# The first MLP's second matrix: three quarters with stationary activations, a sum by tokens, and a turn back to features

## The chip, the core and the metric

The kernel runs on one core of one Trainium2 chip. The metric is the device time of one launch in microseconds (us), weights read from HBM included. The input is one sequence of 256 tokens with 2048 features, in float32.

## What is computed

A two-layer trunk. Each layer has a mixer and an MLP, both behind a modulated norm, and both added to the stream through a gate. The change touches the MLP of layer 0 alone:

```
h = rms_norm(x, norm_mlp_w) * (1 + sc2) + sh2        # 256 x 2048
a = relu(h @ w1) ** 2                                # w1: 2048 x 8192
x = x + g2 * (a @ w2)                                # w2: 8192 x 2048, one gate g2 per feature
```

The gate is a number for each output feature, the same for all tokens. So the gate may be put on the whole sum `a @ w2` or on each part of it.

## The kernel before

The stream `x` lies in SBUF by features: four tiles `x[0..3]` of 128 partitions x 4 x 256, a partition for a feature, the 256 tokens along the row. All weights come from HBM in loads of 1 MB (128 x 2048 float32), each the work of one *item*. To keep float32 precision at TensorE's faster format, each half of a load is split into a high part `wh` (ScalarE, a cast, L342) and a low part `wl` (VectorE, load minus high part, L346); activations are split likewise when they are made. An item multiplies high by high, high by low and low by high.

There are three kinds of item. `c_item` (L592) holds 128x128 of weights stationary and moves the activations: its `wh` products move high and low activations together (512 columns), its `wl` products the high ones alone (256 columns). The output has features on partitions, as `x` has. `a_item` (L554) holds 128x128 of activations stationary and moves 512 columns of weights; its output has tokens on partitions. `b_item` is not used in the MLP.

The MLP (`mlp`, L1516) has four passes `f` over 2048 of the 8192 hidden features. In each pass eight blocks of two `c_item`s make the hidden features (first matrix, evacuated by `relu2`), then eight blocks of two `c_item`s multiply them by the second matrix. After each such block `residual` (L951) adds the gated PSUM tile to `x` with four VectorE instructions (L958). One pass is thus 32 items, 16 of each matrix.

Beside this, the vectors of modulation (`sc`, `sh`, `g` of later norms) are made on VectorE: `mod_job` (L452) loads 1 MB into the same four `raw` buffers as the weights and multiplies and sums it with one instruction (L466). In layer 0's MLP 0.377 of such steps is put out per tick (L1561), four ticks to an item, which comes to about three of these loads to four of weights.

The order of the work is set as the program is written: `emit` (L252) loads item n+1 and then writes the products of item n; `tick` (L236) steps queued generators between pieces of an item, those in `self.fast` first, those in `self.bg` in turn. A scheduler then fixes one order for each engine and for SyncE's DMA queue, and each engine goes through its row strictly in that order: an instruction that waits holds all behind it. There are four `raw` buffers, four `wh` halves, five `wl` halves (two items' worth) and two large PSUM tiles.

Of the kernel before, what the change touches and what calls it, by code (L numbers as in the profile page):

```python
# [10 lines left out]
F32 = mybir.dt.float32  # L11
# [3 lines left out]
ALU = mybir.AluOpType  # L15
# [3 lines left out]
P = 128  # L19
D = 2048  # L20
SEQ = 256
# [91 lines left out]
class Trunk:  # L113
# [332 lines left out]
    def mod_start(self, layer):  # L446

        mix, mlp = ("mix", layer), ("mlp", layer)
        for v, key in enumerate((mix, mix, mix, mlp, mlp, mlp)):
            self.mod[v % 3, key] = self.const([P, 16], f"mod{layer}{v}")  # L450
# [497 lines left out]
        return get  # L948


    def residual(self, ps, cb, key, last, final=False, fs=(0, 1)):  # L951

        nc = self.nc
        self.need(2, key, 2 * cb + 2)
        g, x, b = self.mod[2, key], self.x[cb // 2], cb % 2
        for f in fs:
            for n in range(2):
                self.last = nc.vector.scalar_tensor_tensor(x[:, 2 * b + f], ps[:, f, n], g[:, 2 * cb + f : 2 * cb + f + 1], x[:, 2 * b + f], op0=ALU.mult, op1=ALU.add)  # L958
# [557 lines left out]
    def mlp(self, layer, acts, after=None):  # L1516

        nc = self.nc
        w1, w2 = self.i["w1"][layer], self.i["w2"][layer]
        NF = DFF // 2048  # L1520

        def relu2(ps, early):
            p = self.unit(F32R, [P, 2, 2, SEQ])
            lo = self.s2([P, 2, SEQ], tag="rs")
            nc.scalar.copy(lo, ps[:, :, 1])  # L1525
            nc.vector.tensor_tensor(lo, ps[:, :, 0], lo, op=ALU.add)  # L1526
            if early:
                self.early_add(lo)
            yield
            rl = self.s2([P, 2, SEQ], tag="rl")  # L1530
            nc.scalar.activation(rl, lo, AF.Relu)
            nc.scalar.activation(rl, rl, AF.Square)
            self.split(rl, p[:, :, 0], p[:, :, 1])
            return p

        half = lambda n: acts(n // 2)[0][n % 2]
        for f in range(NF):
            a = {}

            def sink(ps, cb, f=f, a=a):  # L1540
                a[cb % 8] = self.evac(relu2(ps, cb == 0), 1)
                if cb == 7:
                    self.mlp_rate(layer)

            if f == 0:
                self.first_blocks(w1, (0, 1, 2), half, sink)
            for cb in range(3 if f == 0 else 0, 8):
                self.c_blocks(w1, (f * 8 + cb,), half, sink)
            for cb in range(8):
                if f == NF - 1 and cb == 6:  # L1550
                    self.still = 4
                self.c_blocks(w2, (cb,), lambda n, a=a: a[n].finish(),
                              lambda ps, cb, fs=(0, 1), f=f: self.residual(ps, cb, ("mlp", layer), f == NF - 1, layer == 1 and f == NF - 1, fs), f * 2,
                              f == NF - 1 and cb == 7)
        if after is None:
            self.drain()
        else:
            self.early_item(after)

    def mlp_rate(self, layer):  # L1560
        self.rate = 0.377 if layer == 0 else 0.25  # L1561
# [226 lines left out]
def pack(inputs):  # L1788

    f = lambda n: np.asarray(inputs[n])  # L1790
    c = np.ascontiguousarray

    def chunks(w, width=512):
        k, n = w.shape
        nk = 2048 // width
        return c(w.reshape(k // (nk * P), nk, P, n // width, width).transpose(0, 3, 2, 1, 4)).reshape(k // (nk * P), n // width, P, 2048)
# [16 lines left out]
        "w1": np.stack([chunks(w, 256) for w in f("mlp_w1")]), "w2": np.stack([chunks(w, 256) for w in f("mlp_w2")]),  # L1813
    }


# [27 lines left out]
```

## Time and profile before

| | us |
|---|---|
| median of 3 runs | 2692.02 (2691.77 to 2692.03) |
| the profiled execution's own time | 2691.54 |
| its span, first to last instruction | 2689.8 |
| TensorE busy in the span | 2635.2 (98%) |
| VectorE busy | 2151.9 (80%) |
| ScalarE busy | 1348.2 (50%) |
| layer 0's MLP, second norm to end of the fourth pass | about 580 to 1290 of the span |

Times inside the span count from its first instruction. A row of the view by line names line, engine, operation, output<-inputs, count, busy time and the mean of one; `PEld` is the loading of a stationary operand, `SPq` the queue on which SyncE issues DMAs. In the timeline, neighbouring like instructions are drawn together: start, length of the stretch, what, xcount, and in brackets the idle time before and who ended it. The view by windows gives, for a stretch, the busy time of each engine, TensorE's granted clock (PEclk), the mean busy share of the 16 DMA engines and the rate.

### The profile page before, as it was taken

How to read it: one execution, taken by the hardware profiler on the slowest of the kernel's cores; microseconds unless marked ns; L12 is line 12 of the kernel's file. 1: busy time of each engine (PE TensorE's matmuls, PEld its weight loads, DVE VectorE, ACT ScalarE, POOL GpSimd, SP SyncE). 2: the span in 40 equal slices, each digit the busy share in tenths (PEclk: the TensorE clock that was granted, in tenths of full speed). 3: DMA queues.
4: the chain of work that ended last, by engine and by line, in shares of the span. 5: the costliest groups of instructions: out<-in, count | busy, mean ns of one | idle time of the engine just before them, and what ended most of it. 6: DMA issues, size and time to landing. Idle time of an engine off the chain costs nothing.

```text
span 2689.8 us, 40012 instructions
## 1 busy us (share of the span) xinstructions
PE 2635.2 (98%) x15834; PEld 2324.1 (86%) x15834; DVE 2151.9 (80%) x3106; ACT 1348.2 (50%) x1990; POOL 24.3 (1%) x98
## 2 busy tenths in 40 slices
PE   5999999999999999999999999999999999999999
PEld 4887989988888888888888888888888888888888
DVE  7998998997888888889889876888797855555554
ACT  3445455456345354454556544655455354453452
POOL 1000000000000000000000000000000000000000
PEclk9999999999999999999999999999999999999999
DMA  9986487868899898988566655655567855555553
GB/s 344 352 327 234 170 307 275 322 235 293 313 345 328 328 332 330 333 331 312 179 207 220 219 204 185 207 175 188 208 236 293 325 188 188 188 188 188 191 193 134
DMA packets 100459, 680.08 MB, mean 253 GB/s; under 512 B 11184, under 2 KB 14512, under 8 KB 19376
## 3 DMA queue, kind: packets, MB, share of 16 engines
q1 hardware_dynamic: 95376, 669.07, 68.6%
q10 hardware_dynamic: 4896, 8.46, 1.0%
q8 instruction: 124, 2.03, 0.3%
q14 instruction: 63, 0.52, 0.1%
HBM read 675.33 MB, written 2.16 MB: 252 GB/s over the span
## 4 chain that ended last, share of the span: by engine, by line
PE 90%; DVE 7%; ACT 2%; issue 1%; DMA 1%; DVEq 0%; SPq 0%; ACTq 0%
PE pw L332 71%; PE pg L332 12%; PE pm L335 3%; PE pm L332 2%; DVE wl L346 2%; DVE mraw L466 2%; PE pm L339 1%; DVE u L1619 0%; ACT wh L342 0%; DVE hf L893 0%; DVE u L1017 0%; DMA raw<-in_w_ab_dram 0%; ACT pm L1075 0%; DVE u L896 0%; ACT pm L1218 0%
## 5 line engine op out<-in xcount | busy, mean ns | idle before, releaser
L346 DVE TENSOR_TENSOR wl<-raw,wh 128x1024 fp32r<-128x1024 f32 x870 | 1053.8, 1223 | 433.4 <-ACT wh L342 430.9
L342 ACT CAST wh<-raw 128x1024 fp32r<-128x1024 f32 x870 | 905.0, 1050 | 980.8 <-PE pw L332 676.6
L332 PE MATMUL pw<-u,wh 128*128 128x512 f32 x5584 | 1318.8, 391 | 2.6 <-DVE u L896 1.3
L332 PEld LDWEIGHTS pw<-u,wh 128*128 128x128 f32 x5584 | 1032.5, 188 | 209.3 <-issue 1.9
L332 PEld LDWEIGHTS pw<-u,wl 128*128 128x128 f32 x5584 | 702.1, 191 | 21.0 <-DVE wl L346 1.1
L332 PE MATMUL pw<-u,wl 128*128 128x256 f32 x5584 | 711.0, 283 | 0.7 <-DVE wl L346 0.7
L466 DVE SCALAR_TENSOR_TENSOR mraw<-mraw,crow 128x2048 f32<-128x2048 f32 x192 | 438.8, 2287 | 8.6 <-DMA mraw<-in_mod_dram 8.4
L332 PE MATMUL pg<-wh,u 128*128 128x512 f32 x864 | 282.1, 398 | 0.0
L332 PEld LDWEIGHTS pg<-wh,u 128*128 128x128 f32 x864 | 162.0, 188 | 33.2 <-issue 1.0
L958 DVE SCALAR_TENSOR_TENSOR x<-pw,mod,x 128x256 f32<-128x256 f32 x352 | 161.9, 480 | 32.4 <-PE pw L332 30.0
L332 PE MATMUL pg<-wl,u 128*128 128x512 f32 x432 | 169.7, 393 | 0.4 <-DVE wl L346 0.2
L332 PE MATMUL pg<-u,wh 128*128 128x256 f32 x672 | 124.5, 286 | 0.0
L332 PEld LDWEIGHTS pg<-u,wh 128*128 128x128 f32 x672 | 105.5, 192 | 0.3
L332 PEld LDWEIGHTS pg<-wl,u 128*128 128x128 f32 x432 | 81.3, 188 | 18.2 <-DVE wl L346 1.9
L332 PE MATMUL pg<-u,wl 128*128 128x256 f32 x336 | 95.6, 284 | 0.1
L332 PE MATMUL pm<-u,wh 128*128 128x256 f32 (+1 forms) x340 | 64.1, 292 | 19.2 <-ACT wh L342 19.2
L332 PEld LDWEIGHTS pm<-u,wh 128*128 128x128 f32 x340 | 54.3, 199 | 20.3 <-ACT wh L342 20.0
L332 PEld LDWEIGHTS pg<-u,wl 128*128 128x128 f32 x336 | 64.4, 192 | 0.3 <-DVE wl L346 0.3
L1017 DVE SCALAR_TENSOR_TENSOR u<-pad,cst,u 128x256 f32<-128x256 f32 x144 | 61.6, 481 | 1.0 <-ACT u L1011 0.7
L1525 ACT COPY rs<-pw 128x512 f32<-128x512 f32 x64 | 36.8, 576 | 34.5 <-PE pw L332 34.5
L895 ACT ACTIVATE u<-hf,mod 128x256 fp32r<-128x256 f32 x64 | 29.3, 501 | 47.2 <-DVE hf L893 47.2
L1526 DVE TENSOR_TENSOR rs<-pw,rs 128x512 f32<-128x512 f32 x64 | 43.9, 686 | 9.9 <-ACT rs L1525 9.9
(298 smaller groups left out, 1520.5 us busy)
## 6 DMA issues: line engine op xcount, KB each, us to landing
raw<-in_w_dram SPq DMA_DIRECT2D x256, 1024.0 KB, 5.4
mraw<-in_mod_dram SPq DMA_DIRECT2D x192, 1024.0 KB, 6.3
raw<-in_w_ab_dram SPq DMA_DIRECT2D x56, 1024.0 KB, 6.3
raw<-in_w_ssd_dram SPq DMA_DIRECT2D x48, 1024.0 KB, 4.8
raw<-in_w_sz_dram SPq DMA_DIRECT2D x32, 1024.0 KB, 4.9
raw<-in_wo_ssd_dram SPq DMA_DIRECT2D x32, 1024.0 KB, 4.9
raw<-in_wo_ab_dram SPq DMA_DIRECT2D x16, 1024.0 KB, 6.0
sE<-sd_rowd ACTq DMA_DIRECT2D x32, 256.0 KB, 3.9
```

The costliest lines, as they stand in the source:

```text
L332: return self.nc.tensor.matmul(o, a, b, start=start, stop=stop, skip_group_check=True)
L335: self.nc.tensor.matmul(o, lhsT, rhs, start=True, stop=True, skip_group_check=True)
L339: return self.nc.tensor.transpose(o, a, self.anti if flip else self.ident[:k, :k])
L342: a = self.nc.scalar.copy(hi, src)
L346: b = self.nc.vector.tensor_tensor(lo, src, hi.bitcast(F32), op=ALU.subtract)
L466: x = nc.vector.scalar_tensor_tensor(raw, raw, 1.0, self.crow, op0=ALU.mult, op1=ALU.mult, accum_out=t[:, f : f + 1])
L895: nc.scalar.activation(hi, h[:, f], AF.Identity, bias=shift[:, col])
L958: self.last = nc.vector.scalar_tensor_tensor(x[:, 2 * b + f], ps[:, f, n], g[:, 2 * cb + f : 2 * cb + f + 1], x[:, 2 * b + f], op0=ALU.mul ...
L1017: nc.vector.scalar_tensor_tensor(h, pad[:, f, 1 + q : 257 + q], w[:, q, j : j + 1], h, op0=ALU.mult, op1=ALU.add)
L1525: nc.scalar.copy(lo, ps[:, :, 1])
L1526: nc.vector.tensor_tensor(lo, ps[:, :, 0], lo, op=ALU.add)
```

## The change

Of layer 0's second matrix, passes 0, 1 and 2 are done with `a_item`s (`w2_sums`): four groups `n` of 512 output features, each over four items and one PSUM tile. Pass 3 stays with `c_item`s and `residual`, and layer 1 stays as it was. The weights of passes 0 to 2 are packed 512 wide (`w2a`) and those of pass 3 256 wide (`w2b`).

The ungated sums of the three passes are kept by tokens, in the SBUF tiles of `x` itself (`tok` is another view of them). For this `x` is copied to HBM once, in pass 0 (`save_x`, four DMAs). Pass 0's sums are copied into the tiles by ScalarE, those of passes 1 and 2 added by VectorE (`add_sums`). Once group `n` of pass 2 is summed, `to_features(n)` runs as a background task: four VectorE transposes (32x32 squares inside 128x256), eight DMAs that put the squares into HBM in pieces of 128 bytes, one DMA that brings the saved `x[n]` back, eight DMAs that read the turned sums in pieces of 1 KB (`xz`), and four VectorE instructions that gate them and add them to `x[n]`. All DMAs go on SyncE's queue.

```diff
+    def save_x(self):
+        self.kept = [self.dram_p.tile([P, 4, SEQ], F32, tag=f"xk{n}", name=f"x_kept{n}") for n in range(4)]
+        for n in range(4):
+            self.nc.sync.dma_start(self.kept[n], self.x[n])
+            yield
...
+    def add_sums(self, ps, n, first):
+        for t in range(2):
+            if first:
+                self.nc.scalar.copy(self.tok(n)[:, t], ps[t])
+            else:
+                self.nc.vector.tensor_tensor(self.tok(n)[:, t], ps[t], self.tok(n)[:, t], op=ALU.add)
+
+    def to_features(self, n, key):
...
+        for t in range(2):
+            ys.append(self.s2([P, 512], tag="xy"))
+            for h in range(2):
+                c = slice(256 * h, 256 * h + 256)
+                nc.vector.transpose(ys[t][:, c], self.tok(n)[:, t, c])
+            yield
+        for t in range(2):
+            for q in range(4):
+                nc.sync.dma_start(scr[:, :, 4 * t + q], ys[t][32 * q : 32 * q + 32].rearrange("p (m i) -> p m i", i=32))
+        nc.sync.dma_start(self.x[n], self.kept[n])
+        for _ in range(5):
+            yield
+        cells = scr.rearrange("j (f a) b i -> j f a (b i)", a=4)
+        zs = [self.s2([P, 2, SEQ], tag="xz") for _ in range(2)]
+        for a in range(4):
+            for h in range(2):
+                nc.sync.dma_start(zs[h][32 * a : 32 * a + 32], cells[:, 2 * h : 2 * h + 2, a])
+        for _ in range(4):
+            yield
+        for f in range(4):
+            x = self.x[n][:, f]
+            nc.vector.scalar_tensor_tensor(x, zs[f // 2][:, f % 2], self.mod[2, key][:, 4 * n + f : 4 * n + f + 1], x, op0=ALU.mult, op1=ALU.add)
...
+            if layer == 0 and f < NF - 1:
+                self.w2_sums(self.i["w2a"], f, NF, lambda n, a=a: a[n].finish(), ("mlp", layer))
+                continue
...
+    def w2_sums(self, w, f, nf, act, key):
+        for n in range(4):
...
+            def after(n=n, ps=ps):
+                self.add_sums(ps, n, f == 0)
+                if f == nf - 2:
+                    self.turned.append(self.back(self.to_features(n, key)))
+            for k in range(4):
+                self.a_item(get, w[4 * f + k, n], lambda k=k: ([act(2 * k), act(2 * k + 1)], None), k == 0, k == 3, after if k == 3 else None)
```

The orders below are of pass 2 (the third), around its middle. Rows of the changed program carry its own line numbers (L968 is `add_sums`, L980 the transposes, L984, L985 and L992 the DMAs of `to_features`, L997 its gated add); the number behind a tile's name tells tiles of one name apart.

TensorE before, one block of the second matrix (two items): first the `wh` products (512 columns) and the `wl` products (256 columns) of one load, then those of the next, 64 matmuls in all.

```order
L332 MATMUL pw_9923<-u_8956,wh_9868 128x512 x4
L332 MATMUL pw_9923<-u_9055,wh_9868 128x512 x4
L332 MATMUL pw_9923<-u_9153,wh_9872 128x512 x4
L332 MATMUL pw_9923<-u_9252,wh_9872 128x512 x4
L332 MATMUL pw_9923<-u_8956,wl_9869 128x256 x4
L332 MATMUL pw_9923<-u_9055,wl_9869 128x256 x4
L332 MATMUL pw_9923<-u_9153,wl_9873 128x256 x4
L332 MATMUL pw_9923<-u_9252,wl_9873 128x256 x4
```

TensorE now, the first half of the first item of group 2 (two halves make an item of 24 matmuls, all with 512 columns).

```order
L332 MATMUL pg_9662<-wh_9614,u_8649 128x512
L332 MATMUL pg_9662<-wl_9615,u_8649 128x512
L332 MATMUL pg_9662<-wh_9614,u_8649 128x512 x2
L332 MATMUL pg_9662<-wl_9615,u_8649 128x512
L332 MATMUL pg_9662<-wh_9614,u_8649 128x512 x2
L332 MATMUL pg_9662<-wl_9615,u_8649 128x512
L332 MATMUL pg_9662<-wh_9614,u_8649 128x512 x2
L332 MATMUL pg_9662<-wl_9615,u_8649 128x512
L332 MATMUL pg_9662<-wh_9614,u_8649 128x512
```

An item has the same columns as before in 24 matmuls instead of 32, and its second matmul already reads `wl`.

VectorE before, at the middle of pass 2. The block `pw_9923` uses the loads `raw_9866` and `raw_9913`; the loads after it are `raw_9959` and `raw_10007`.

```order
L346 TENSOR_TENSOR wl_9962<-raw_9959,wh_9961 128x1024
L346 TENSOR_TENSOR wl_9966<-raw_9959,wh_9965 128x1024
L466 SCALAR_TENSOR_TENSOR mraw_9993,mod_131<-mraw_9993,crow 128x2048
L474 TENSOR_TENSOR mod_131<-mod_131,cst 128x4
L958 SCALAR_TENSOR_TENSOR x_80<-pw_9923,mod_128,x_80 128x256 x4
L346 TENSOR_TENSOR wl_10010<-raw_10007,wh_10009 128x1024
```

VectorE now, at the same place. The PSUM tile `pg_9483` is group 1, whose last load is `raw_9573`; `raw_9612` is the first load of group 2.

```order
L346 TENSOR_TENSOR wl_9576<-raw_9573,wh_9575 128x1024
L346 TENSOR_TENSOR wl_9580<-raw_9573,wh_9579 128x1024
L968 TENSOR_TENSOR x_80<-pg_9483,x_80 128x512 x2
L980 STREAM_TRANSPOSE xy_9670<-x_80 128x256 x2
L980 STREAM_TRANSPOSE xy_9679<-x_80 128x256
L466 SCALAR_TENSOR_TENSOR mraw_9595,mod_131<-mraw_9595,crow 128x2048
L980 STREAM_TRANSPOSE xy_9679<-x_80 128x256
L997 SCALAR_TENSOR_TENSOR x_79<-xz_9563,mod_128,x_79 128x256 x2
L997 SCALAR_TENSOR_TENSOR x_79<-xz_9564,mod_128,x_79 128x256 x2
L346 TENSOR_TENSOR wl_9615<-raw_9612,wh_9614 128x1024
```

Before, the low parts of the next load (`wl_9962`, `wl_9966`) stand ahead of the instruction that reads the finished PSUM tile; now the low part of the next load (`wl_9615`) stands behind it, and behind the transposes, one modulation step and the gated add of group 0. At the other three groups of pass 2, and at all four of pass 1, the low parts of one load more still stand ahead of the add.

SyncE's queue before, at the middle of pass 2.

```order
L509 DMA raw_9913<-in_w_dram 128x2048
L463 DMA mraw_9940<-in_mod_dram 128x2048
L509 DMA raw_9959<-in_w_dram 128x2048
L463 DMA mraw_9993<-in_mod_dram 128x2048
L509 DMA raw_10007<-in_w_dram 128x2048
```

SyncE's queue now, when group 2 is summed: the eight stores of 512 pieces of 128 bytes, the saved `x[2]`, one load of weights (`raw_9885`, the third item after the sum), eight reads of `xz` (the first four shown), and behind all eight the next load, `raw_9930`.

```order
L463 DMA mraw_9883<-in_mod_dram 128x2048
L984 DMA x_turned_9848<-xy_9849 512x1x32 x4
L984 DMA x_turned_9848<-xy_9858 512x1x32 x4
L985 DMA x_81<-x_kept_6165 128x1024
L509 DMA raw_9885<-in_w2a_dram 128x2048
L992 DMA xz_9920<-x_turned_9848 32x2x256
L992 DMA xz_9921<-x_turned_9848 32x2x256
L992 DMA xz_9920<-x_turned_9848 32x2x256
L992 DMA xz_9921<-x_turned_9848 32x2x256
```

Seventeen DMAs have come between loads that stood next to each other, and some wait: the stores for the transposes, the first `xz` read for all eight stores to have landed. A DMA also waits until the one issued eight places ahead of it has landed, since eight semaphores go round.

More of the change, by code (lines that the diff above doesn't have):

```diff
@@ L1518, in mlp @@
         nc = self.nc
-        w1, w2 = self.i["w1"][layer], self.i["w2"][layer]
+        w1, w2 = self.i["w1"][layer], self.i["w2" if layer else "w2b"]
         NF = DFF // 2048
@@ L1541, in sink @@
                 a[cb % 8] = self.evac(relu2(ps, cb == 0), 1)
+                if cb == 3 and layer == f == 0:
+                    self.turned = []
+                    self.back(self.save_x())
                 if cb == 7:
@@ L1548, in mlp @@
                 self.c_blocks(w1, (f * 8 + cb,), half, sink)
+            if layer == 0 and f < NF - 1:
+                self.w2_sums(self.i["w2a"], f, NF, lambda n, a=a: a[n].finish(), ("mlp", layer))
+                continue
+            if layer == 0:
+                for t in self.turned:
+                    if t in self.bg:
+                        self.bg.remove(t)
+                    t.finish()
             for cb in range(8):
```

18 lines of the change are left out of this document (16 added, 2 removed).

## The prediction

> **What bounds the kernel now.** I read the page first, for the engine that sets the span.
>
> ```profile
> PE 2635.2 (98%) x15834; PEld 2324.1 (86%) x15834; DVE 2151.9 (80%) x3106; ACT 1348.2 (50%) x1990; POOL 24.3 (1%) x98
> PE 90%; DVE 7%; ACT 2%; issue 1%; DMA 1%; DVEq 0%; SPq 0%; ACTq 0%
> ```
>
> TensorE is busy 98% of the span and 90% of the chain that ended last. Shares are means, so next comes the view by windows, for the MLP of layer 0, and there the waits by total.
>
> ```profile
> 620.00:1280.00 660.00, 660.00 (x3799) 584.39 (x3799) 563.68 (x634) 316.76 (x377) 0.00 (x0) 1.00 0.89 326
> 1060.00:1180.00 120.00, 120.00 (x696) 106.43 (x695) 103.23 (x115) 54.02 (x63) 0.00 (x0) 1.00 0.90 331
> 20.00:60.00 40.00, 21.27 (x150) 20.60 (x151) 35.06 (x54) 10.60 (x16) 0.00 (x0) 1.00 0.97 351
> ACT wh L342 <- PE pw L332: 203.9, 113, 4.6
> ACT wh L342 <- DMA raw<-in_w_dram: 29.6, 10, 4.8
> ```
>
> From 620 to 1280 TensorE is never idle, at the full clock (1.00). Two resources stand close behind: VectorE (563.68 of 660) and the DMA engines, busy 0.90 of the time in the last part at 331 GB/s. 351 GB/s at 0.97 is the most that a stretch of this trace shows (a stretch in which TensorE waits), about 363 at a share of 1. ScalarE's casts wait for TensorE to free a buffer (203.9 us), and at ten places for a load (29.6 us): loads come in time, without much to spare. So work saved on TensorE here is saved in full, and a weight that comes late costs in full.
>
> **The items (a gain).** The timeline of TensorE, first two items of the second matrix now, then an item with stationary activations in layer 1.
>
> ```profile
> 872.20 4.00 PE L332 MATMUL pw<-u,wl 128*128 128x256 f32 x32
> 876.03 7.44 PE L332 MATMUL pw<-u,wh 128*128 128x512 f32 x32
> 883.31 4.00 PE L332 MATMUL pw<-u,wl 128*128 128x256 f32 x32
> 1447.13 0.39 PE L332 MATMUL pg<-wl,u 128*128 128x512 f32 x1
> 1447.36 0.62 PE L332 MATMUL pg<-wh,u 128*128 128x512 f32 x2
> 1447.81 0.39 PE L332 MATMUL pg<-wl,u 128*128 128x512 f32 x1
> ```
>
> Two items take 883.31 - 872.20 = 11.11 us, one 5.555. Three matmuls of the other kind take 1447.81 - 1447.13 = 0.68 us, so an item of 24 takes 5.44. The columns are equal; a 256-column matmul costs (876.03 - 872.20) / 32 = 0.120 us against 0.227 for 512, more than half. The gain is 0.115 x 48 items = 5.5 us.
>
> A rule speaks against it. The Trainium skill (TensorE: Matmul & The Clock Gate, § Wait — 56ns, not 53.3ns?) gives a warm matmul N / 2.4 GHz plus about 2.5 ns; by that an item would go from 16 x (215.8 + 109.2) = 5200 ns to 24 x 215.8 = 5179, and the estimate of the gain would be 1.0 us in all. The rows show about 13 ns on each matmul here, so the sum keeps 5.5.
>
> **VectorE's row at the middle of pass 2 (a loss).** The mean durations by line:
>
> ```profile
> L346 DVE TENSOR_TENSOR wl<-raw,wh 128x1024 fp32r<-128x1024 f32 x209 | 250.8, 1222 | 52.0 <-ACT wh L342 51.6
> L466 DVE SCALAR_TENSOR_TENSOR mraw<-mraw,crow 128x2048 f32<-128x2048 f32 x77 | 176.0, 2286 | 0.3 <-DMA mraw<-in_mod_dram 0.3
> L958 DVE SCALAR_TENSOR_TENSOR x<-pw,mod,x 128x256 f32<-128x256 f32 x112 | 51.4, 480 | 18.5 <-PE pw L332 17.7
> L474 DVE TENSOR_TENSOR mod<-mod,cst 128x4 f32<-128x4 f32 x18 | 2.9, 160 | 0.3
> L846 DVE TENSOR_TENSOR ss<-ss,sq 128x256 f32<-128x256 f32 x48 | 20.6, 429 | 0.9
> L1619 DVE TENSOR_TENSOR u<-pg,u 128x512 f32<-128x512 f32 x24 | 15.7, 688 | 0.3 <-PE pg L332 0.3
> ```
>
> The low part of group 2's first load now stands behind the add that reads group 1's PSUM tile, and that add can't begin before TensorE's last matmul of group 1. TensorE's next item needs the low part at its second matmul. So TensorE waits for two adds (2 x 0.69 = 1.4), four transposes, a modulation step (2.3), four gated adds (4 x 0.48 = 1.9) and the low part itself (1.2). No row shows a transpose: 0.16 (L474, the shortest) to 0.48 (L958) bound one; I take 0.43, the row of the same tile shape (L846), 1.7 for four. Sum 8.5, less the first matmul: **8.3 us** of idle TensorE. Only two loads' worth of split weights exist, both used up by then, so nothing hides it.
>
> VectorE's total falls: 96 gated adds go (46.1 us); 16 adds, 16 transposes and 16 gated adds come (11.0 + 6.9 + 7.7 = 25.6). It was not the bound, so that is worth nothing.
>
> **The DMAs of a turn (a loss).** One load's issue on SyncE's queue in a steady stretch, its cast and TensorE's stretch around it, the DMA queues' totals, and times to landing:
>
> ```profile
> 875.13 0.33 SPq L509 DMA_DIRECT2D raw<-in_w_dram  x1
> 881.70 1.05 ACT L342 CAST wh<-raw 128x1024 fp32r<-128x1024 f32 x1 [0.76 <-DVE x L958]
> 887.14 7.44 PE L332 MATMUL pw<-u,wh 128*128 128x512 f32 x32
> q1 hardware_dynamic: 95376, 669.07, 68.6%
> q10 hardware_dynamic: 4896, 8.46, 1.0%
> raw<-in_w_dram SPq DMA_DIRECT2D x256, 1024.0 KB, 5.4
> u<-in_attn_rel_bias_dram SPq DMA_DIRECT2D x2, 512.0 KB, 6.8
> 272.70:274.30 1.60, 1.60 (x9) 1.33 (x7) 1.60 (x4) 1.60 (x4) 0.00 (x0) 1.00 0.92 330
> ```
>
> How early is a load? The one issued at 875.13 is cast from 881.70 into buffers freed by the item that started at 879.67 (half of the 7.28 us from 876.03 on), and used two items later, at 890.8 (half of the stretch from 887.14 on). From issue to use are 15.7 us; less 5.4 to land, 1.05 and 1.22 to split, 8.0 are to spare.
>
> A turn adds to the DMA engines: 4096 pieces of 128 bytes; 512 rows of 1 KB, like those of the bias, which moved in 1.6 us (window 272.7:274.3, rows of 1 KB at 330 GB/s); and the saved tile, 0.52 MB at 363 GB/s, 1.4 us. No row shows a 128-byte piece. Below, at its bytes' share of the full rate, 4096 take 1.4 us; above, at the price of whole 1 KB rows, 8 x 1.6 = 12.8. I take a line through the two queues: 0.686 x 16 x 2689.8 / 95376 = 0.310 us for a mean packet of 7.0 KB and 0.010 x 16 x 2689.8 / 4896 = 0.088 for 1.7 KB give 16 ns and 0.042 ns a byte, 21 ns for 128 bytes, **5.4 us** for 4096 over 16 engines. Four turns make 4 x (5.4 + 1.6 + 1.4) = 34 us in 87 us of items of which the engines had 0.10, 9 us, free.
>
> Now one turn, from TensorE's end T of the group. Adds to T+1.4; stores from the second transpose at 2.3. A load takes 5.4 to land of which 1.05 MB at 363 GB/s are 2.9, so 2.5 go to starting and finishing, half at each end. Pieces through at 2.3 + 1.25 + 5.4 = 9.0, the saved tile at 10.4, the load behind it at 13.3, landed at 14.5, split at 16.8. It is needed two items after T, at 10.9: **5.9 late**. The next load is issued once all eight reads are, and the last two of these wait for the saved tile and that load: issue about 15.2, split 22.9, needed at 16.8 + 5.44 = 22.2, 0.7 late.
> - Group 0: the load behind the reads is the first of group 2; its lateness lies within the 8.3 us above.
> - Group 1: a modulation load is ahead as well, split at 19.7; with the 8.3 it is needed at 19.2: 0.5.
> - Groups 2 and 3: 5.9 + 0.7 = 6.6 each. Within this lies a wait of 1.2 for VectorE (add, transposes, modulation step, low part: 6.7 against 5.44).
>
> Waits in all: 8.3 + 0.5 + 13.2 = **22.0 us**.
>
> Nothing for `save_x`: its 2.1 MB (5.8 us) leave where x is finished, before the loads of the first blocks, and the DMA engines are idle more than half of that stretch:
>
> ```profile
> 580.00:600.00 20.00, 19.13 (x102) 16.54 (x102) 18.25 (x41) 13.96 (x26) 0.00 (x0) 0.91 0.43 157
> 582.00:584.00 2.00, 2.00 (x8) 1.75 (x7) 2.00 (x5) 2.00 (x5) 0.00 (x0) 0.50 0.00 0
> 580.37 0.43 PE L339 MATMUL pm<-ident,rsy 128*128 128x128 f32 x2 [2.22 <-DVE rsy L287]
> ```
>
> Without that cover it would cost up to 5.8. Nothing either for pass 0's copies and pass 1's adds, which have one load split ahead of them. The same rows show a price of waiting: after 2.22 us of idle TensorE the clock stood at 0.50 and the mean of the 20 us at 0.91, so 0.09 x 20 = 1.8 us were lost. I count it for two of the waits, **3.6 us**; behind a third the loads are late anyway, so a slow clock costs nothing more there.
>
> **Sum.** -5.5 + 22.0 + 3.6 = +20.1, on the profiled 2691.54: 2711.6. The median shown is 0.5 above that execution, so 2712.
>
> **Rivals.** Times are again against the median, 2692.0.
> - *Hidden* (the other side): TensorE keeps its gain and the waits vanish, 2686.5. It would happen in pass 2 if the split weights of one more load were ready at the middle and a turn's DMAs fitted into the 8.0 us to spare; it decides once all waits of the pass stay under 5.5 us. For it: VectorE's load falls, and a load is 8.0 early. Against it: VectorE's row alone costs 8.3. Chance 0.05.
> - *VectorE's row alone*: the pieces move so quickly that no load is late. At 1.4 us for them the third load of a turn is late by 1.9 only, which the clock and my rounding can hide: 2692.0 - 5.5 + 8.3 + 1.8 = 2696.6. Against it: DMA engines busy 0.90 of the time, and stores that must first wait for the transposes. Chance 0.14.
> - *Dear pieces*: each costs as much as a 1 KB row, 12.8 us a turn. Each of three turns is 7.4 us later: 2712 + 22 = 2734; at twice that price, 12.8 us more a turn, 2772. For it: each piece goes to its own place in HBM, 1 KB from the next. Against it: the line of the two queues. Chance 0.16.
>
> For the last the Trainium skill has a rule (DMA: Bandwidth & Descriptors, § Specifications): under 512 bytes a transfer is below line rate, since the engine reads, modifies and writes. No run here shows stores of such pieces yet.
>
> **How the numbers follow.** Forecast 0.65, hidden 0.05, VectorE's row alone 0.14, dear pieces 0.16. The forecast's own range goes from pieces at 1.4 us (groups 2 and 3 late by 2.6 each, group 1 not: 2712 - 8.5 = 2703) to 9.1 us, halfway to the dear price (3 x 3.7 more: 2712 + 11 = 2723). To hold 8 in 10 the range reaches to VectorE's row alone below and the first price of dear pieces above: 2695 to 2734. A measurement of this kernel can tell about 0.2%, 5.4 us, from no change: faster holds the first rival, within 0.2% the second, the rest is slower. 0.05, 0.13, 0.82.
>
> **What would show it.** Right: items of pass 0 to 2 at 5.44 us; TensorE idle some 8 us at the middle of pass 2, ended by the low part L346, with the add L968 and the transposes ahead of it; two waits of 5 to 7 us about 11 us after the sums of groups 2 and 3, ended by a cast whose load landed late; the rest of the span as long as before. Wrong: no idle TensorE in pass 2, or waits in passes 0 and 1; a transpose over 1 us; stores of a turn that take over 10 us (dear pieces) or under 3; items of 24 matmuls at 5.5 us or more.

## The result, and the profile after

| | before, us | after, us |
|---|---|---|
| median | 2692.03 (4 runs, 2691.77 to 2694.20) | 2717.45 (4 runs, 2714.66 to 2720.84) |
| the profiled execution's own time | 2691.54 | 2720.84 |

The changed kernel takes 1.0096 of the time before, with a 95% interval of 1.0084 to 1.0109 (the brackets behind a ratio below are such intervals): 25.4 us slower, between the forecast of 2712 and the upper end of its range. The execution that was profiled is the slowest of the four, 3.4 us above their median, so what the traces show adds up to a little more than 25.4. The page of the changed kernel:

```profile
PE 2641.7 (97%) x15450; PEld 2310.2 (85%) x15450; DVE 2135.5 (79%) x3058; ACT 1353.0 (50%) x1998; POOL 24.5 (1%) x98
PE 81%; DVE 10%; DMA 5%; ACT 2%; issue 1%; SPq 1%; ACTq 0%; DVEq 0%
```

TensorE has 384 matmuls fewer, and yet is busy 6.5 us longer. Of the 9 points of the chain that it has lost, DMA took 4 and VectorE 3. To place this, I cut out layer 0's MLP, from the first transpose of its norm to that of the next norm. The view by windows, columns: stretch, its length, busy time of TensorE, weight load, VectorE, ScalarE and GpSimd (count in brackets), granted clock, DMA share, GB/s. Before:

```profile
580.37:1297.37 717.00, 715.46 (x4122) 633.49 (x4122) 610.74 (x718) 350.83 (x429) 0.00 (x0) 1.00 0.86 314
```

After, the same stretch, then the part of it with the turns, then three pieces of that part:

```profile
581.19:1322.87 741.68, 719.74 (x3741) 617.89 (x3739) 592.04 (x668) 354.64 (x437) 0.00 (x0) 0.98 0.85 311
1060.00:1180.00 120.00, 99.60 (x457) 81.24 (x456) 85.94 (x102) 40.88 (x46) 0.00 (x0) 0.91 0.88 312
1069.90:1076.70 6.80, 4.45 (x11) 3.54 (x12) 6.80 (x9) 1.99 (x2) 0.00 (x0) 0.51 0.89 190
1114.30:1121.10 6.80, 4.89 (x11) 3.56 (x12) 3.95 (x6) 2.85 (x3) 0.00 (x0) 0.51 0.81 295
1145.00:1151.80 6.80, 5.35 (x13) 4.23 (x14) 4.78 (x8) 4.99 (x7) 0.00 (x0) 0.51 0.83 305
```

The MLP is 24.7 us longer (741.68 - 717.00); of the 28.9 between the two spans (2718.7 and 2689.8), 0.8 lie ahead of it and 3.4 behind. TensorE is idle 741.68 - 719.74 = 21.9 us, against 1.5 before, and 20.4 of that is in the 120 us of the turns (120.00 - 99.60). The rest is no wait: the clock stood at 0.51 for 6.8 us at each of three waits. The main waits on TensorE's timeline:

```profile
1067.65 0.49 PE L332 MATMUL pg<-wh,u 128*128 128x512 f32 x1 [3.02 <-ACT wh L342]
1072.25 0.80 PE L332 MATMUL pg<-wl,u 128*128 128x512 f32 x1 [4.10 <-DVE wl L346]
1105.33 0.50 PE L332 MATMUL pg<-wl,u 128*128 128x512 f32 x1 [1.25 <-DVE wl L346]
1115.74 0.79 PE L332 MATMUL pg<-wh,u 128*128 128x512 f32 x1 [4.86 <-ACT wh L342]
1117.00 0.80 PE L332 MATMUL pg<-wl,u 128*128 128x512 f32 x1 [0.47 <-DVE wl L346]
1135.78 2.36 PE L332 MATMUL pw<-u,wl 128*128 128x256 f32 x16 [0.50 <-DVE wl L346]
1146.45 6.32 PE L332 MATMUL pw<-u,wh 128*128 128x512 f32 x16 [4.66 <-ACT wh L342]
```

The first two rows are one place, the middle of pass 2: 7.1 us idle, the first part for a high part and the second for the low one. The 4.86 and the 4.66 are the third loads after groups 2 and 3, the 1.25 and the 0.50 VectorE's row behind these groups. A matmul of 0.8 us is one at half speed behind the wait. VectorE at the middle of pass 2:

```profile
1064.67 1.29 DVE L968 TENSOR_TENSOR x<-pg,x 128x512 f32<-128x512 f32 x2 [8.57 <-PE pg L332]
1065.88 1.09 DVE L980 STREAM_TRANSPOSE xy<-x 128x256 f32<-128x256 f32 x3
1066.89 2.25 DVE L466 SCALAR_TENSOR_TENSOR mraw<-mraw,crow 128x2048 f32<-128x2048 f32 x1
1069.07 0.44 DVE L980 STREAM_TRANSPOSE xy<-x 128x256 f32<-128x256 f32 x1
1069.43 1.63 DVE L997 SCALAR_TENSOR_TENSOR x<-xz,mod,x 128x256 f32<-128x256 f32 x4
1070.98 2.35 DVE L346 TENSOR_TENSOR wl<-raw,wh 128x1024 fp32r<-128x1024 f32 x2
```

The row is the one predicted: add, transposes, modulation step, gated add, low part. The first low part is through at about 1072.2, 7.5 us after the add began. SyncE's queue in the turn of group 2, and the DMA engines while the stores go out:

```profile
1101.33 5.26 SPq L984 DMA_DIRECT2D x_turned<-xy  x8
1106.63 0.62 SPq L985 DMA_DIRECT2D x<-x_kept  x1
1107.35 0.39 SPq L509 DMA_DIRECT2D raw<-in_w2a_dram  x1
1108.33 6.53 SPq L992 DMA_DIRECT2D xz<-x_turned  x8
1114.97 0.36 SPq L509 DMA_DIRECT2D raw<-in_w2a_dram  x1
```

```profile
1101.60:1107.00 5.40, 4.16 (x18) 3.10 (x18) 5.40 (x7) 1.25 (x2) 0.00 (x0) 1.00 0.52 97
```

The stores hold SyncE's queue for 5.3 us, 0.66 each, and the reads hold it for 6.5. But the DMA engines are busy only half of the time that the stores take (0.52). The records of single packets show that this is not a few full engines beside idle ones: up to 20 packets run at once, and in 14% of that stretch none does. What is full there is the queue, not the engines. Whether that queue, the engines or VectorE's row makes TensorE wait is what the experiments had to tell.

### The profile page after: what moved, and what is told of

The parts are those of the page before. It is cut to its first block, busy times and chain, and to the rows that moved or that the text cites. A ratio compares the mean times of both kernels' runs of the same rounds, so it can differ in the third digit from the quotient of the medians.

```text
span 2718.7 us, 39304 instructions
## 1 busy us (share of the span) xinstructions
PE 2641.7 (97%) x15450; PEld 2310.2 (85%) x15450; DVE 2135.5 (79%) x3058; ACT 1353.0 (50%) x1998; POOL 24.5 (1%) x98
## 4 chain that ended last, share of the span: by engine, by line
PE 81%; DVE 10%; DMA 5%; ACT 2%; issue 1%; SPq 1%; ACTq 0%; DVEq 0%
PE pw L332 55%; PE pg L332 19%; PE pm L335 3%; DVE wl L346 3%; DVE mraw L466 3%; PE pm L332 2%; DMA mraw<-in_mod_dram 1%; PE pm L339 1%; DMA raw<-in_w2a_dram 1%; DMA raw<-in_wo_ab_dram 1%; DMA raw<-in_w_ab_dram 1%; ACT wh L342 1%; DVE x L1008 0%; DVE u L1699 0%; SPq L984 0%
## 5 line engine op out<-in xcount | busy, mean ns | idle before, releaser
L342 ACT CAST wh<-raw 128x1024 fp32r<-128x1024 f32 x870 | 905.1, 1051 | 998.1 <-PE pw L332 545.3
L332 PE MATMUL pw<-u,wh 128*128 128x512 f32 x4816 | 1144.0, 392 | 6.8 <-ACT wh L342 4.7
L332 PEld LDWEIGHTS pw<-u,wh 128*128 128x128 f32 x4816 | 892.1, 189 | 185.9 <-ACT wh L342 5.1
L332 PEld LDWEIGHTS pw<-u,wl 128*128 128x128 f32 x4816 | 607.3, 191 | 23.4 <-DVE wl L346 4.9
L332 PE MATMUL pw<-u,wl 128*128 128x256 f32 x4816 | 617.1, 283 | 3.2 <-DVE wl L346 3.1
L332 PE MATMUL pg<-wh,u 128*128 128x512 f32 x1632 | 522.8, 396 | 8.1 <-ACT wh L342 8.1
L332 PEld LDWEIGHTS pg<-wh,u 128*128 128x128 f32 x1632 | 308.1, 189 | 72.9 <-ACT wh L342 9.3
L332 PE MATMUL pg<-wl,u 128*128 128x512 f32 x816 | 321.3, 394 | 7.5 <-DVE wl L346 7.1
L332 PEld LDWEIGHTS pg<-wl,u 128*128 128x128 f32 x816 | 154.4, 189 | 42.5 <-DVE wl L346 11.0
L1008 DVE SCALAR_TENSOR_TENSOR x<-pw,mod,x 128x256 f32<-128x256 f32 x256 | 117.5, 478 | 16.6 <-PE pw L332 14.9
```

The source lines that it names most:

```text
L332: return self.nc.tensor.matmul(o, a, b, start=start, stop=stop, skip_group_check=True)
L342: a = self.nc.scalar.copy(hi, src)
```

## The experiments

All times are medians beside the kernel before on the same chip (2691.1 to 2691.7 there); "norm to norm" is the stretch cut out above, its length and TensorE's busy time.

### No turn (e1)

```diff
-                if f == nf - 2:
-                    self.turned.append(self.back(self.to_features(n, key)))
```

> The turn is left out (no transposes, stores, restoring of x, reads or gated adds; x holds bare token sums afterwards); items, sums and the saving of x stay. Theory (the items gain 5.5 us, the turn costs the 20.4 us of idle TensorE and about 9.5 us of slow clock): before - 5.5 = 2686.5, 2685.5 to 2688, no idle TensorE over 1 us between 1040 and 1180, clock 1.00 there. Rival A (the sums or the saving of x cost part of the loss): 2692 or more. Rival B (items do not gain): 2691 to 2693.

Measured: 2686.57 (2684.57 to 2689.25, 10 runs), 0.998 [0.9971, 0.999]. Norm to norm:

```profile
579.70:1291.00 711.30, 709.75 (x3738) 613.49 (x3738) 580.70 (x636) 355.90 (x437) 0.00 (x0) 1.00 0.86 316
```

Idle is back at 1.5 us. The items alone bring 715.46 - 709.75 = 5.7 us, `save_x` and the sums cost nothing, and the whole loss is the turn: 20.4 us of waits, and 719.74 - 709.75 = 10.0 us by which the same matmuls take longer.

### The turn without its DMAs (e2)

The eight stores, the restoring DMA and the reads are left out; the gated add reads the transposed tile.

```diff
-                nc.sync.dma_start(scr[:, :, 4 * t + q], ys[t][32 * q : 32 * q + 32].rearrange("p (m i) -> p m i", i=32))
-        nc.sync.dma_start(self.x[n], self.kept[n])
...
-                nc.sync.dma_start(zs[h][32 * a : 32 * a + 32], cells[:, 2 * h : 2 * h + 2, a])
+        zs = [y.rearrange("p (f t) -> p f t", f=2) for y in ys]
```

> Transposes and gated adds stay (the adds read the transposed tile, so features are not put back); stores, restoring and reads are left out, and with them the order on VectorE changes: no transposes stand between the add of group 1 and the first low part of group 2. Theory (waits come from loads queued behind the turn's DMAs, and from VectorE's order that came with them): 2686.5 to 2690. Rival A (VectorE's added work itself makes TensorE wait, whatever the order): 2695 to 2702.

Measured: 2686.83 (2686.08 to 2689.11, 10 runs), 0.9983 [0.9973, 0.9992], as without a turn; norm to norm 711.50, busy 709.95. VectorE's added work by itself costs nothing. That does not clear its place in the row, since with the DMAs gone the scheduler's order at the middle moved too; e5 looks at that.

### Stores in long pieces (e3)

Each store writes 32 rows of 2 KB of the scratch tensor instead of 512 pieces; the squares are no longer put in their turned places.

```diff
+        rows = scr.rearrange("j m b i -> j (m b i)").rearrange("j (q c) -> j q c", q=8)
-                nc.sync.dma_start(scr[:, :, 4 * t + q], ys[t][32 * q : 32 * q + 32].rearrange("p (m i) -> p m i", i=32))
+                nc.sync.dma_start(rows[:, 4 * t + q], ys[t][32 * q : 32 * q + 32])
```

> The eight stores of a turn keep their bytes, their number and their place in the queue, but each writes 32 rows of 2 KB in place of 512 pieces of 128 bytes, so that what is read back is not turned rightly. Theory (the stores hold SyncE's queue for as long as their pieces take to issue, 0.66 us a DMA): issue 0.35 us or less a DMA, a block of 5.3 us becomes 2.8 or less, the loads behind come 2.5 us earlier at three places: 2710, 2703 to 2713. Rival A (a price for each DMA whatever its pieces): the block stays over 4.5 us, 2716 to 2719. Rival B (the pieces' time on the DMA engines): the issue stays at 0.66 us, but the landings come 3 us earlier and with them the reads: 2708 to 2713.

Measured: 2707.51 (2706.98 to 2707.85, 4 runs), 1.006 [1.0045, 1.0075]. SyncE's queue in the same turn, and the middle of pass 2:

```profile
1098.58 3.64 SPq L985 DMA_DIRECT2D x_turned<-xy  x8
1103.30 5.77 SPq L993 DMA_DIRECT2D xz<-x_turned  x8
1072.20 0.79 PE L332 MATMUL pg<-wl,u 128*128 128x512 f32 x1 [7.09 <-DVE wl L346]
```

The pieces are worth 10 of the 25 us. The waits behind groups 2 and 3 fell from 4.9 and 4.7 to 1.9 and 1.6. The queue gave 1.8 us of that behind group 2, where the load follows the first store by 4.2 us instead of 6.0. It then took 6.0 us to land instead of 7.2, so that in all it is there 3.0 us earlier. A store still took 0.45 us, not the 0.35 expected. The reads hold the queue nearly as before (5.8 us), and the middle still costs 7.1 us, now all put down to the low part.

### The turn's DMAs on GpSimd's queue (e4)

All 17 DMAs of a turn go from `nc.sync` to `nc.gpsimd`; the edit is that word.

> The turn's 17 DMAs are issued on GpSimd's queue; weight loads stay on SyncE's. With it the first low part of group 2 comes ahead of the add of group 1 on VectorE. Bytes and pieces are the same. Theory (a load waits on SyncE's queue behind stores that wait for transposes and are issued at 0.66 us each, and behind reads that wait for landings): waits under 5 us, 2687 to 2694. Rival A (the DMA engines: 8.4 us of added work a turn): the loads at groups 2 and 3 stay 5 us late, 2703 to 2712. Rival B (VectorE's row alone counts): 2717.5 - 8.3 - 3.4 = 2706.

Measured: 2755.58 (2753.49 to 2758.50, 4 runs), 1.0235 [1.022, 1.025]: a miss, much slower. Waits and timelines of GpSimd's queue, VectorE and TensorE:

```profile
POOL x_turned L984 <- issue: 87.9, 25, 6.2
DVE x L997 <- DMA xz<-x_turned: 63.6, 4, 17.3
1051.83 0.66 POOL L984 DMA_DIRECT2D x_turned<-xy  x1 [5.01 <-issue]
1077.14 0.62 POOL L984 DMA_DIRECT2D x_turned<-xy  x1 [1.81 <-issue]
1085.36 1.67 DVE L997 SCALAR_TENSOR_TENSOR x<-xz,mod,x 128x256 f32<-128x256 f32 x4 [17.30 <-DMA xz<-x_turned]
1090.44 0.80 PE L332 MATMUL pg<-wl,u 128*128 128x512 f32 x1 [16.20 <-DVE wl L346]
```

GpSimd needs 2.4 us for one store of 512 pieces at best and up to 6.9 (the issue shown in front of the brackets, plus the gap). So the first turn's eight stores take 31.8 us (1045.96 to the restoring DMA at 1077.76), VectorE reaches the gated add 17 us before its data, and the low parts behind it make TensorE wait 16.2. The 1.81 fell where VectorE was idle, the 5.01 where it was busy throughout; but one gap of 5.54 fell into a stretch in which VectorE did nothing either, so what stretches the issue stays open. The Trainium skill (DMA: Bandwidth & Descriptors, § SWDGE vs HWDGE vs iDMA) says that GpSimd makes its descriptors in software, piece by piece, and writes them to SBUF state from which VectorE locks it out while it runs in its two-port mode. The price per store agrees with the first half (2.4 us at best, against 0.66 on SyncE's queue), and the gap of 5.54 shows that the second is not all of it.

### The add behind the next low parts (e5)

```diff
-                self.nc.vector.tensor_tensor(self.tok(n)[:, t], ps[t], self.tok(n)[:, t], op=ALU.add)
+                self.put_behind(self.nc.vector.tensor_tensor(self.tok(n)[:, t], ps[t], self.tok(n)[:, t], op=ALU.add), self.low)
```

`self.low` is the last low part written so far. At the middle of pass 2 this puts the add and the transposes behind the low parts that TensorE needs next.

> One change of order: in pass 1 and 2 the adds of a group's sums are put behind the low part of the load split last, which moves the add of group 1 and its transposes behind the two low parts of group 2's first load; queues stay. Theory: the 4.1 us of idle TensorE that VectorE's row ends goes, the 3.0 us ended by the late cast stay; the clock may win a window of 3.4: 2710 to 2713.5. Rival A (the DMA engines only): 2717, within 2. Rival B (VectorE's row is the whole wait at the middle): 2717.5 - 8 - 3.4 = 2706.

Measured: 2719.26 (2717.53 to 2721.68, 4 runs), 1.01 [1.0085, 1.0115]: no gain, a miss. TensorE at the middle:

```profile
1067.74 0.49 PE L332 MATMUL pg<-wh,u 128*128 128x512 f32 x1 [3.42 <-ACT wh L342]
1087.47 0.79 PE L332 MATMUL pg<-wh,u 128*128 128x512 f32 x1 [5.98 <-ACT wh L342]
```

The wait for the low part fell to 0.8 us, but the one for the high part stayed, and 6.0 us appeared at 1087.5, where the third load after group 1 is now late: with add and transposes moved back, the turn's stores go out 5.3 us later (1071.98 instead of 1066.66), and that load, queued behind them, lands at 1086.27 instead of 1084.17, while TensorE comes to it 2.9 us sooner. What was won at the middle was lost there.

### Reads put out later (e7)

The pause between the stores and the reads is 12 steps instead of 5.

```diff
-        for _ in range(5):
+        for _ in range(12):
```

> The reads of a turn come seven steps of the background task later, behind one to three further loads on SyncE's queue (at group 0 one, at groups 1 to 3 three weight and modulation loads or more); stores and bytes as before. Theory (reads that wait in the queue for the stores' landings hold up the load behind them by 3 to 4 us): the eight reads take 3 us in place of 6.5, waits fall from 20.4 to about 10, with one clock window less 2704, 2698 to 2710. Rival A (DMA engines' added work): 2715 to 2719. Rival B (the stores' block alone delays loads): 2714 to 2718.

Measured: 2719.88 (2719.46 to 2722.87, 4 runs), 1.011 [1.0093, 1.0127]: no gain. The stores had long landed, and yet:

```profile
1085.02 0.33 SPq L509 DMA_DIRECT2D raw<-in_w2a_dram  x1
1088.62 0.33 SPq L463 DMA_DIRECT2D mraw<-in_mod_dram  x1
1089.00 7.82 SPq L992 DMA_DIRECT2D xz<-x_turned  x8
1096.92 0.37 SPq L509 DMA_DIRECT2D raw<-in_w2a_dram  x1
```

The records of single DMAs show it: reads 1 to 6 were issued by 1092.4, the seventh at 1093.19, when the load of 1085 had landed (1093.17), the eighth at 1096.52, when that of 1088.6 had (1096.50). Each is the DMA eight places ahead. With eight unfinished at most, eight reads in a row must run into the two DMAs before them, wherever they stand.

### Spaced out (e8), and fewer modulation loads beside it (e9)

In e8 a step of the program stands between any two DMAs of a turn. e9 also moves modulation loads out of pass 2:

```diff
+                yield
...
-                if cb == 7:
-                    self.mlp_rate(layer)
+                if cb % 8 == 7:
+                    self.mlp_rate(layer, f)
...
-        self.rate = 0.377 if layer == 0 else 0.25
+        self.rate = (0.45 if f < 2 else 0.26) if layer == 0 else 0.25
```

> The turn's DMAs are issued one to a step of the background task, and the reads and gated adds wait six ticks, so that loads stand between the stores and between the reads on SyncE's queue (the eight stores of group 0 still stand together); all DMAs and bytes as before. Theory (the wait is the queue's order): waits under 5 us, 2687 to 2696. Rival A (DMA engines: 23 us of added work beside loads that keep them 0.9 busy): 2700 to 2712. Rival B (stores wait for the transposes and hold the queue in any order): 2705 to 2717.

> As the spaced turn, and the modulation loads go at a rate of 0.45 through passes 0 and 1 and 0.26 behind, instead of 0.377 throughout; as many have been loaded by the end of the layer. Theory (queue order alone): as the spaced turn, within 2 us. Rival A (the DMA engines have too little free time for the turns): 4 us or more faster than the spaced turn, 2686.5 to 2692, as 0.12 x 140 / 5.4 = some 3 loads of 1 MB fewer fall into the turns' stretch, 9 us of DMA time.

Measured: e8 2716.51 (2715.84 to 2717.64, 4 runs), 1.0094 [1.0079, 1.0109]; e9 2728.62 (2727.57 to 2729.20, 4 runs), 1.0139 [1.0123, 1.0154]. Two misses. Norm to norm they are alike, 740.68 and 740.75, though between 1040 and 1180 e9 issued 11 modulation loads and e8 15; the 12 us more of e9 were lost in layer 1, whose order had moved. A small DMA between loads can still wait for the load eight places ahead (a read of e8 went out at 1135.91, 2.9 us behind the DMA before it, when such a load had landed at 1135.89). That this is why fewer loads brought nothing is argued, not shown: in both runs one of the longest waits, 4.3 us, ends with a cast that stands in ScalarE's row behind other work, as in e12 below.

### Two reads instead of eight, and the add behind (e10)

e5's edit, with the scratch tensor in an order in which one DMA reads 128 partitions:

```diff
+        scr = self.dram_p.tile([16, 32, 8, 32], F32, tag=f"xt{n}", name=f"x_turned{n}")
...
-        for a in range(4):
-            for h in range(2):
-                nc.sync.dma_start(zs[h][32 * a : 32 * a + 32], cells[:, 2 * h : 2 * h + 2, a])
+        for h in range(2):
+            nc.sync.dma_start(zs[h], cells[:, 2 * h : 2 * h + 2])
```

> Two edits: the scratch rows are laid so that the eight reads of a turn become two of the same bytes and pieces (1 KB), and the adds stand behind the last low part as in the run with that edit alone. New theory (SyncE's queue may have eight DMAs unfinished; the last reads of a turn wait for the landing of the load issued eight DMAs before, and the next load waits behind them; VectorE's row at the middle is as late as that load, so that either edit alone gains nothing): the reads leave SyncE in under 2 us in place of 6.5, the wait at the middle falls from 8 to 2 us or less, the 5 us behind the stores' block at groups 2 and 3 stay: 2704 to 2711. Rival A (the reads wait for the stores' landings, however many they are): reads still 4 us or more on the queue, 2714 to 2719. Rival B (the DMA engines' added work): 2714 to 2719.

Measured: 2707.02 (2704.68 to 2708.19, 4 runs), 1.0057 [1.0041, 1.0074], within what the theory gave. Norm to norm 732.44, busy 718.71.

```profile
1096.73 4.10 SPq L984 DMA_DIRECT2D x_turned<-xy  x8
1102.32 0.88 SPq L991 DMA_DIRECT2D xz<-x_turned  x2
```

The reads hold the queue for 0.9 us instead of 6.5, and the waits at the middle are 0.6 and 1.2 us, where e5's edit alone had left 4.2. Behind groups 2 and 3 it left 3.7 and 3.1, less than the 5 expected. Two reads without that edit were not run, so what each of the two is worth is not separated. The eight stores, of as many pieces, took 4.1 us instead of 5.3: their places in HBM have changed too.

### Seven DMAs a turn (e11), and all of it later (e12)

e11 on e10: both transposed tiles in one, so that four stores of 512 pieces of 256 bytes carry a turn. e12 on e11: transposes and gated adds also `put_behind`, with more steps before each (3, 2, 4 and 9).

```diff
-        scr = self.dram_p.tile([16, 32, 8, 32], F32, tag=f"xt{n}", name=f"x_turned{n}")
+        scr = self.dram_p.tile([16, 32, 4, 64], F32, tag=f"xt{n}", name=f"x_turned{n}")
...
+        for q in range(4):
+            nc.sync.dma_start(scr[:, :, q].rearrange("m j e -> j m e"), y[32 * q : 32 * q + 32].rearrange("p m t i -> p m (t i)"))
```

> As the run with two reads and the adds behind, and the transposes of both token halves are written side by side, so that a turn has four stores of 512 pieces of 256 bytes in place of eight of 512 pieces of 128; the gated adds become eight of half the columns; seven DMAs a turn with the restoring of x, bytes as before; one buffer fewer for small tiles. New theory (queue: issue time by pieces and eight unfinished DMAs): the stores' block is 2.6 us in place of 5.3, so the third load after groups 2 and 3 is 3 us late at most: 2692 to 2701. Rival B (the DMA engines' added work: 0.90 busy before, and as many bytes): 2708 to 2717. Rival C (stores hold the queue while they wait for the transposes, whatever their number): 5 us stay at groups 2 and 3, 2704 to 2711.

> As the run with seven DMAs, and every step of a turn later: transposes and gated adds stand behind the low part of the load split last, the stores go out some two ticks behind the transposes, so that a load or two that the stores held up before is ahead of them on SyncE's queue, and the reads and gated adds follow four and nine ticks later. Bytes and number of DMAs as in that run. Theory (what is left there is the load queued behind stores that wait for the transposes, and the low part behind add, transposes and a modulation step): waits under 2 us, no clock window, 2687 to 2693. Rival B (the DMA engines, at a share of 0.95 to 1.01 in two of the stretches of that run, are what is left): 2697 to 2704.

Measured: e11 2704.77 (2701.19 to 2706.90, 4 runs), 1.005 [1.0035, 1.0065]; e12 2704.70 (2701.61 to 2706.59, 5 runs), 1.0048 [1.0035, 1.0062]. Both miss the theory's range. The total of e11 lies in that of Rival C, but the 5 us at groups 2 and 3 that this rival named are 1.8 and 1.9. Norm to norm: e11 728.28, busy 717.15; e12 726.88, busy 715.99. In e11 four stores hold the queue for 2.2 us, and no wait is above 2.5; in e12 one of 4.3 is left, for a cast:

```profile
1140.11 0.58 ACT L1574 COPY rs<-pw 128x512 f32<-128x512 f32 x1 [4.44 <-PE pw L332]
1142.78 0.62 ACT L342 CAST u<-rl 128x512 fp32r<-128x512 f32 x1
1143.30 3.88 ACT L342 CAST wh<-raw 128x1024 fp32r<-128x1024 f32 x4
1144.39 5.52 PE L332 MATMUL pw<-u,wh 128*128 128x512 f32 x16 [4.32 <-ACT wh L342]
```

By the order of loads and casts, the load of that cast had landed at 1137.70. It stands in ScalarE's row behind the evacuation of the block before (L1574 to L342 `u`), which waits for TensorE's last matmul of that block; so these 4.3 us are an order of instructions, not a late load. A stretch of the turns in e12:

```profile
1060.00:1100.00 40.00, 37.78 (x157) 29.91 (x156) 31.98 (x44) 14.04 (x15) 0.00 (x0) 0.96 1.01 390
1080.00:1100.00 20.00, 18.49 (x74) 14.60 (x73) 16.07 (x21) 6.03 (x7) 0.00 (x0) 0.91 1.00 404
```

With the queue free, the DMA engines are full: a share of 1.0 at 390 to 404 GB/s. Of e12's two ranges, that of the rival that named them came nearest; it ends 0.7 us below the measured time. And though idle time is down to 11 us, the busy time is still 6.2 us above that of e1.

### Fewer modulation loads beside the turns (e13)

e12, with 14 modulation loads instead of 24 issued from the end of pass 2's first matrix to the end of pass 3's, and as many by the end of the MLP (86):

```diff
-                if cb == 7:
-                    self.mlp_rate(layer)
+                if cb % 8 == 7:
+                    self.mlp_rate(layer, f)
...
-        self.rate = 0.377 if layer == 0 else 0.25
+        self.rate = (0.45, 0.45, 0.2, 0.47)[f] if layer == 0 else 0.25
```

> As the later run, and the modulation loads are moved out of the turns' stretch: a rate of 0.45 through passes 0 and 1, 0.2 from the end of pass 2's first matrix, 0.47 from the end of pass 3's, in place of 0.377; 13 loads of 1 MB there in place of 24, as many in all by the end of the layer. Theory (what is left are the DMA engines, at 1.01 and 1.00 of their time from 1060 to 1100): the norm of layer 0's MLP to the next norm 714 us or less against 726.9, waits under 3 us, 2688 to 2696. Rival (queue order and the eight unfinished DMAs are what is left): 724 us or more between the norms, 2701 to 2706. Should layer 1 lose by the other order of its loads, as in the spaced run with another rate (norm to norm as without it, 12 us lost behind), the time between the norms decides, not the total.

Measured: 2692.14 (2690.56 to 2695.64, 11 runs), 1.0004 [0.9995, 1.0013]. Norm to norm 715.20, 1.2 above what the theory had named as its sign and 8.8 below the rival's; busy 712.72. The whole stretch of the turns in e12 and in e13, and the one of e13 that answers to the first above:

```profile
1040.00:1180.00 140.00, 130.65 (x626) 109.60 (x625) 113.09 (x149) 53.93 (x61) 0.00 (x0) 0.96 0.92 337
1040.00:1180.00 140.00, 139.37 (x704) 119.03 (x703) 108.60 (x143) 63.59 (x72) 0.00 (x0) 1.00 0.87 321
1060.00:1100.00 40.00, 40.00 (x178) 33.15 (x177) 29.09 (x44) 15.30 (x15) 0.00 (x0) 1.00 0.95 369
```

TensorE is idle 0.6 us in 140 instead of 9.4, at the full clock. With the loads 12.6 us went, 11.7 of them between the norms. That the DMA engines were what was left fits, since their share in the fullest stretch fell from 1.01 to 0.95, but the run doesn't show it alone: each load moved away also takes its place out of SyncE's queue and its 2.3 us out of VectorE's row, and the order of the rows is another, so that the 4.3 us behind ScalarE's evacuation are gone as well. A smaller move of the same kind had brought the MLP nothing while the queue was blocked (e9). In the MLP this version is 1.8 us faster than the kernel before; 2.5 are lost behind it, of which one stretch of 3.4 us at a clock of 0.50, from 1411.1, makes some 1.7. As a whole it equals the kernel before, no more, and no version with a whole turn beat it.

## Why the prediction was right, by its steps

The direction and the places of the waits were right, and the time lies in the range: 5.5 gained, 22.0 of waits and 3.6 of clock, +20.1 in all, came out as 5.7, 20.4 and 10.0. That sum is 24.7, the MLP's share of the loss; the 3.4 us behind the MLP were not forecast and not traced. Part of the nearness is luck: the price of the pieces came out by another mechanism than the one it was worked out from, and waits forecast 1.6 us too long make up for some of the clock's 6.4.

- **Items: right.** 5.7 us against 5.5 (e1). The 2.5 ns per matmul of the Trainium skill (TensorE: Matmul & The Clock Gate, § Wait — 56ns, not 53.3ns?) would have given 1.0; the rows' 13 ns decide.
- **VectorE's row at the middle of pass 2: right in size, half right in cause.** Predicted 8.3 us of idle TensorE, measured 7.1. A transpose was 0.4 us, as taken. The first 3.0 of it wait for the late load behind group 0's reads, as the sentence on group 0 has it ("its lateness lies within the 8.3 us above"). What the prediction didn't see is that the row and the loads can't be taken one by one: with the row moved, 4.2 us stayed at the middle and 6.0 came up at the third load after group 1 (e5), where it was 0.8 before (0.5 forecast). With two reads besides, both shrank, to 1.8 and 3.1 (e10).
- **The turn's DMAs: the step that failed, in its mechanism.** The 5.4 us for 4096 pieces were put on the 16 DMA engines at 21 ns a piece. The stores did take 5.3 us, but on SyncE's queue, where one of 512 pieces took up to 0.66 us to issue, with the engines busy 0.52; that the two numbers agree is luck. In the trace a 128-byte packet holds an engine for 11 ns (median; 11.8 on average), so that 4096 are 3.0 us of 16 engines. Long pieces (e3) gave back 1.6 us of the block and 1.2 of the landing of the load behind it. What sets the 0.66 stays open: as many pieces took 0.51 in e10, and the restoring DMA, 128 rows, took 0.62 right behind the stores. The waits behind group 2 came out as 1.25 for VectorE's row (1.2 forecast), 4.86 for the third load and 0.47 for the low part after it, 6.6 in all as forecast; behind group 3 as 0.50 and 4.66, 5.2 instead of 6.6.
- **The reads: held as said, for a longer time.** The eight-place wait was named for the last two reads; with it the reads held the queue for 6.4 to 9.6 us a turn. Putting them later (e7) or spacing them (e8) did not help, fewer DMAs did (e10, e11).
- **The DMA engines' load: named, and not the first limit.** The 34 us of work against 9 free show as a limit only once the queue was clear: a share of 1.0 in e12, and the time won in e13, which moved other work as well.
- **The clock: mis-sized, 3.6 against 10.0.** I counted two waits at 1.8. There were three stretches of 6.8 us at half speed, and the claim that a slow clock costs nothing more behind a third wait was wrong: behind the last one TensorE went on without waiting, so what the clock took came back nowhere. The Trainium skill (TensorE: Matmul & The Clock Gate, § What's actually happening) has a free-running window of 3413 ns after which the gate decides; 6.8 us are two of these, which agrees. Shorter waits cost too: in e11, with none above 2.5 us, the clock stood at 0.50 for 6.8 us from 1080.0 and for 3.4 us from 1110.7, 5.1 us of work lost. TensorE was busy 7.4 us longer there than in e1; the other 2.3 are open.
- **Nothing for `save_x` and the sums: right** (e1 has both).
- **The rivals.** *VectorE's row alone* falls, since late loads end the waits of 3.0, 4.9 and 4.7 us. *Dear pieces*, and the rule of the Trainium skill (DMA: Bandwidth & Descriptors, § Specifications) that pieces under 512 bytes go below line rate, were not what decided: 97 GB/s is low, which agrees, but the engines were half idle. *Hidden* needed what e13 had to build.

Open: what sets the time of a store's issue on SyncE's queue; what stretches GpSimd's (e4); which part of e13's gain is the DMA engines'; why e13 is busy 3.0 us longer than e1 in the MLP, at the full clock; and the 12 us of e9 in layer 1, which were seen but not traced to an edit.

## What to carry to other kernels

Count DMAs, and the pieces in each, not only their bytes: on an in-order queue with eight unfinished at most, a handful of small ones waits for the big loads before them and holds back the big loads behind. When several resources are late at the same place, removing one may show nothing (e5), so remove them together before judging any. A detour through HBM needs room on the queue, on the DMA engines and in VectorE's row all at once; here a gain of 5.7 us just paid for it when all three had been made.

## What the runs showed of the hardware

- SyncE issued a DMA of 128 rows in 0.33 us in a steady stretch and in 0.62 right behind eight stores. Stores of 512 pieces of 128 bytes, eight in a row, took 0.66 each, and 0.51 with other places in HBM (e10); GpSimd took 2.4 to 6.9 for one (e4).
- At waits of 4.7 to 7.1 us TensorE's clock stood at 0.51 for 6.8 us; in e11 it also fell to 0.50 at waits of 1.8 to 2.5 us, for 3.4 and 6.8.
- No DMA on SyncE's queue was issued before the one eight places ahead had landed, in any of the 729 of e7; two of its reads went out right behind such a landing (1093.19 after 1093.17, 1096.52 after 1096.50).
- The DMA engines moved 404 GB/s at a share of 1.00 over 20 us (e12), above the 363 that I had worked out from the kernel before.
